# Remainders of the mixers' second-group weight pieces: VectorE in place of GpSimd

## The chip, the cores and the metric

The kernel runs on one core of one Trainium2 chip. A time is the device time of one execution in microseconds (us). Several executions are timed and their median is given; the profile is of one further execution, which has a time of its own.

## What is computed

The reference is one inference step of a decoder trunk with two layers (width 1024), for 1024 prompt tokens and 8 sample tokens that go through the same weights. Layer 0 mixes the tokens by dilated window attention, layer 1 by a pooling mixer. After each of them stands a gated channel mixer (ConvGLU) of hidden width 2816:

```python
def conv_glu(h, gate_prefix, w_in, conv_w, conv_b, w_out):
    u = h @ w_in
    gate, val = u[..., :D_FF], u[..., D_FF:]
    ext = jnp.concatenate([gate_prefix, gate], axis=1)
    S = h.shape[1]
    conv = conv_b + ext[:, 0:S] * conv_w[0]
    for j in range(1, CONV_WIDTH):
        conv = conv + ext[:, j:j + S] * conv_w[j]
    y = (jax.nn.silu(conv) * val) @ w_out
```

The pooling mixer takes trailing means over 2, 4, 8 and 16 tokens in four groups of channels, subtracts the token itself, and applies a linear map per group and a scale per channel. Every sub-layer begins with an RMSNorm and ends with a residual add. All is in float32.

## The kernel before

**Layout.** Channels lie on the 128 partitions, tokens on the free axis. The 1032 tokens are cut into chunks of 352, 336 and 344 columns (`CHUNKS`, line 21), and for the channel mixers into two groups (`GROUPS`, line 23): the first has chunks 0 and 1 (688 columns), the second has chunk 2 (344 columns: 336 prompt tokens and 8 sample tokens).

**Three products for one.** A float32 product is made of three matmuls in the fast float32 format: operands are split into a rounded part (`hi`) and the remainder (`lo`), and `accumulate` (line 115) adds hi·hi, hi·lo and lo·hi in PSUM.

**Weight pieces.** All weights come as one list of pieces of 128 x 1024 values (512 KB), in the order of use (line 56 on). SyncE's queue loads a piece into `w_raw` (line 88); ScalarE copies it to the rounded `w_hi` (line 99); GpSimd subtracts to make `w_lo` (line 100; two pieces at the very start are subtracted by VectorE, line 953); then the load of a later piece is issued, which goes into a buffer that the subtraction has released. `w_get` hands out the next piece, and `w_ahead(3)` splits pieces up to three ahead of the one in use. In the mixers there are four buffers each of `w_raw`, `w_hi` and `w_lo`, so that a new piece is split into the buffer that the piece four before it leaves.

**The channel mixers.** `steps` (lines 60 to 71) writes the order of their work out by hand: for each layer and each of the two groups, 22 up-projection steps `up`, of two pieces each (gate and value), with six `down` steps between them. The whole list of weights is gone through once for each group. In a step `up` (line 1079), a gate piece is multiplied with the normed tokens (`hh`, `hl`), ScalarE takes it out of PSUM (line 1097) and starts the convolution (line 1112), VectorE ends it (lines 1114 and, for the sample tokens, 1117), ScalarE applies SiLU (line 1101), VectorE multiplies with the value piece (line 1104), ScalarE rounds to `gh` (line 1105) and GpSimd subtracts to make `gl` (line 1106). A step `down` (line 1134) multiplies four (or two) such tiles with w_out, and VectorE adds the sums to the residual `xT` (line 1052). For the first group, a piece serves 24 matmuls in each of two chunks; for the second, 24 matmuls of 344 columns.

**What runs beside it.** `later` (line 166) puts small tasks of norms and of the pooling into a queue with due times in TensorE's modelled time, and `accumulate` sets them off between matmuls. So the order of each engine's instructions is fixed when the program is written, and each engine goes through its own in order. The pooling of chunks 0 and 1 (class `Pooling`, line 1166: `normed`, `sums`, `centred`, `high`, `low`; VectorE, with ScalarE for the rounding) is put in while layer 0's second group of tokens runs, with the costs of lines 1198 to 1203 as due times (modelled at one column of a matmul per 1/2400 us, line 122), and its projection (`project`, line 1262; two pieces) comes after the third `down` of that group.

Of the kernel before, what the change touches and what calls it, by code (L numbers as in the profile page):

```python
# [11 lines left out]
F32 = mybir.dt.float32  # L12
# [35 lines left out]
def trunk(ctx: ExitStack, tc: tile.TileContext, a, out):  # L48
    nc = tc.nc
# [6 lines left out]
    pieces = [a["w_qkv"][i] for i in range(72)] + [a["w_o"][h, i] for h in range(2) for i in range(4)]  # L56
# [4 lines left out]
    steps = []  # L61
# [9 lines left out]
        steps += [("up", x, 0) for x in halves[1:] if halves.index(x) == halves.index(at) + 1] + [("down", at, 5)]  # L71

    third = len(pieces) + 4
    for kind, (layer, _), which in steps:
        if kind == "up":
            pieces += [a["w_in"][layer, 2 * which + i] for i in range(2)]
        elif kind == "down":
            pieces += [a["w_out"][layer, DOWN[which][2] + i] for i in range(DOWN[which][1])]
        else:
            pieces += [a["w_pool"][i] for i in range(2)]  # L80
    raws, split, nxt, more = {}, {}, [0, 0, 0], [None]

    def w_load(n):
        while nxt[0] <= min(n, len(pieces) - 1):
            i = nxt[0]
            p = more[0] if i >= third and i % 4 > 1 else wpool
            raws[i] = p.tile([128, 1024], F32, name="w_raw", tag="w_raw", bufs=2)
            nc.sync.dma_start(out=raws[i], in_=pieces[i])
            nxt[0] += 1

    def w_split(n, eng=None, load=True):
        while nxt[1] <= min(n, len(pieces) - 1):
            i = nxt[1]
            w_load(i)
            p = more[0] if more[0] is not None and i % 4 > 1 else wpool
            hi = p.tile([128, 1024], F32R, name="w_hi", tag="w_hi", bufs=2)
            lo = p.tile([128, 1024], F32R, name="w_lo", tag="w_lo", bufs=2)
            raw = raws.pop(i)
            nc.scalar.activation(hi, raw, AF.Copy)  # L99
            (eng or nc.gpsimd).tensor_sub(lo, raw, hi.bitcast(F32))  # L100
            split[i] = (hi, lo)
            nxt[1] += 1
            if load:
                w_load(i + (4 if i >= third else 2))

    def w_get():
        i = nxt[2]
        nxt[2] += 1
        w_split(i)
        return split.pop(i)  # L110

    def w_ahead(k, load=True):
        w_split(nxt[2] - 1 + k, load=load)
# [168 lines left out]
    with ExitStack() as ph:  # L282
# [587 lines left out]
        for f in squares(0):  # L870
            f()
        w_split(0)
        ahead = squares(1)
        for f in ahead[:2] + [norms[0].stats, norms[0].spread] + ahead[2:6]:
# [537 lines left out]
```

## Time and profile before

| | |
|---|---|
| median of 3 runs | 2903.01 us (2902.28 to 2905.36) |
| time of the profiled execution | 2902.76 us |
| its span, first to last instruction | 2900.8 us |
| TensorE (PE) busy | 2786.3 us, 96% |
| VectorE (DVE) busy | 1629.2 us, 56% |
| ScalarE (ACT) busy | 1357.9 us, 47% |
| GpSimd (POOL) busy | 1409.8 us, 49% |
| of that, `w_lo` subtractions (line 100) | 848.5 us in 346 instructions |
| mean granted TensorE clock | 0.988 |

A row that says "A <- B" tells that A waited and that B ended the wait. L100 is line 100 of the kernel. PE is TensorE's matmuls and PEld its loads of weights into the array. A matmul's duration overlaps with that of its neighbours, so a row's mean for one matmul is more than its share of the time. The time of an execution is about 2 us longer than its span. Stretches are given in us from the start of the span.

### The profile page before, as it was taken

What the parts mean: (1) busy time and instruction counts of PE and PEld (TensorE: products, weight loads), DVE (VectorE), ACT (ScalarE), POOL (GpSimd) and SP (SyncE); (2) the same over time, 40 slices, a digit from 0 to 9 for tenths busy, and PEclk for the clock granted to TensorE, in tenths of its full rate; (3) what the DMA queues carried; (4) which work ended last, traced back from release to release, by engine and by line L of the source; (5) the groups of instructions that cost most, each with busy time, mean ns of one, the idle gap of its engine ahead of it and who ended that gap; (6) DMA issues with size and microseconds to landing.
All of it is one profiled execution on the core that took longest, in us unless ns stands there. A gap on an engine that the chain in (4) does not pass through costs nothing.

```text
span 2900.8 us, 46721 instructions
## 1 busy us (share of the span) xinstructions
PE 2786.3 (96%) x18109; PEld 2741.8 (95%) x18109; DVE 1629.2 (56%) x3196; ACT 1357.9 (47%) x2748; POOL 1409.8 (49%) x999
## 2 busy tenths in 40 slices
PE   6999999999999999999999999988899999999998
PEld 5999999999999999889999999988899999999998
DVE  6666756675666566765323334787756333435555
ACT  5565665566556655534222323445442333334443
POOL 4235443545354435445434434566753443445785
PEclk9999999999999999999999999999999999999999
DMA  3234333433343324438222222333332226223543
GB/s 117 58 85 124 95 86 87 122 90 91 82 128 94 87 86 145 139 95 106 67 73 73 66 73 73 109 103 108 119 103 66 73 67 81 67 72 98 182 139 102
DMA packets 203949, 277.80 MB, mean 96 GB/s; under 512 B 70272, under 2 KB 154096, under 8 KB 203728
## 3 DMA queue, kind: packets, MB, share of 16 engines
q1 hardware_dynamic: 203680, 274.80, 34.3%
q8 instruction: 142, 2.33, 0.3%
q14 instruction: 79, 0.65, 0.1%
q10 hardware_dynamic: 48, 0.02, 0.0%
HBM read 251.89 MB, written 23.34 MB: 95 GB/s over the span
## 4 chain that ended last, share of the span: by engine, by line
PE 77%; DVE 13%; ACT 3%; issue 3%; POOL 2%; DMA 1%; SPq 0%; DVEq 0%; ACTq 0%; POOLq 0%
PE mm L120 68%; PE o L489 2%; DVE k L408 2%; PE s L462 1%; POOL w_lo L100 1%; PE pt L475 1%; DVE conv L1117 1%; DVE conv L1114 1%; DVE x L399 1%; ACT w_hi L99 1%; PE s L455 1%; DVE x L397 1%; DVE sums L1225 1%; DVE sc L634 1%; PE spv L768 1%
## 5 line engine op out<-in xcount | busy, mean ns | idle before, releaser
L120 PE MATMUL mm<-hh,w_hi 128*128 128x352 f32 (+2 forms) x4064 | 1343.9, 331 | 13.9 <-ACT w_hi L99 6.9
L120 PE MATMUL mm<-hh,w_lo 128*128 128x352 f32 (+2 forms) x4064 | 1308.8, 322 | 10.4 <-POOL w_lo L100 10.4
L120 PE MATMUL mm<-hl,w_hi 128*128 128x352 f32 (+2 forms) x4064 | 1308.0, 322 | 2.4 <-DVE hl L255 2.4
L100 POOL TENSOR_TENSOR w_lo<-w_raw,w_hi 128x1024 fp32r<-128x1024 f32 x346 | 848.5, 2456 | 672.1 <-ACT w_hi L99 649.3
L120 PEld LDWEIGHTS mm<-hh,w_hi 128*128 128x128 f32 x4064 | 772.7, 190 | 20.7 <-ACT w_hi L99 7.5
L120 PEld LDWEIGHTS mm<-hh,w_lo 128*128 128x128 f32 x4064 | 771.2, 190 | 13.1 <-POOL w_lo L100 13.1
L120 PEld LDWEIGHTS mm<-hl,w_hi 128*128 128x128 f32 x4064 | 773.2, 190 | 4.7 <-DVE hl L255 3.9
L1114 DVE SCALAR_TENSOR_TENSOR conv<-gate,convp,conv 128x336 f32<-128x336 f32 (+1 forms) x176 | 253.6, 1441 | 428.6 <-ACT conv L1112 412.2
L99 ACT ACTIVATE w_hi<-w_raw 128x1024 fp32r<-128x1024 f32 x348 | 363.4, 1050 | 259.9 <-PE mm L120 240.1
L120 PE MATMUL mm<-gh,w_hi 128*128 128x352 f32 (+2 forms) x1056 | 340.8, 323 | 7.6 <-DVE conv L1104 6.3
L120 PE MATMUL mm<-gh,w_lo 128*128 128x352 f32 (+2 forms) x1056 | 340.1, 322 | 3.5 <-POOL w_lo L100 3.5
L120 PE MATMUL mm<-gl,w_hi 128*128 128x352 f32 (+2 forms) x1056 | 339.8, 322 | 0.6 <-POOL gl L1106 0.6
L1052 DVE TENSOR_TENSOR x<-x,mm 128x352 f32<-128x352 f32 (+2 forms) x312 | 157.1, 511 | 257.1 <-PE mm L120 256.5
L467 ACT ACTIVATE p<-p,st 128x128 f32<-128x128 f32 (+1 forms) x384 | 170.0, 443 | 202.4 <-DVE st L464 201.7
L1106 POOL TENSOR_TENSOR gl<-conv,gh 128x352 fp32r<-128x352 f32 (+2 forms) x132 | 124.5, 944 | 238.1 <-ACT gh L1105 233.4
L120 PEld LDWEIGHTS mm<-gh,w_hi 128*128 128x128 f32 x1056 | 199.6, 189 | 9.3 <-DVE conv L1104 7.6
L120 PEld LDWEIGHTS mm<-gh,w_lo 128*128 128x128 f32 x1056 | 200.1, 189 | 4.4 <-POOL w_lo L100 4.4
L120 PEld LDWEIGHTS mm<-gl,w_hi 128*128 128x128 f32 x1056 | 199.8, 189 | 1.1 <-POOL gl L1106 1.1
L480 DVE TENSOR_TENSOR phl<-pt,phl 128x512 fp32r<-128x512 f32 (+1 forms) x192 | 104.6, 545 | 164.2 <-ACT phl L479 163.1
L368 ACT ACTIVATE raw<-mm 128x336 f32<-128x336 f32 (+1 forms) x216 | 144.5, 670 | 102.5 <-PE mm L120 99.1
L1101 ACT ACTIVATE conv<-conv 128x688 f32<-128x688 f32 (+1 forms) x88 | 55.9, 635 | 275.1 <-DVE conv L1114 137.2
L1097 ACT ACTIVATE gate<-mm 128x352 f32<-128x352 f32 (+2 forms) x132 | 59.8, 454 | 224.1 <-PE mm L120 222.5
(190 smaller groups left out, 3190.3 us busy)
## 6 DMA issues: line engine op xcount, KB each, us to landing
w_raw<-in_w_in SPq DMA_DIRECT2D x176, 512.0 KB
w_raw<-in_w_out SPq DMA_DIRECT2D x88, 512.0 KB
w_raw<-in_w_qkv SPq DMA_DIRECT2D x72, 512.0 KB
x<-qd SPq DMA_DIRECT2D x48, 256.0 KB
kc<-in_cache_k SPq DMA_DIRECT2D x48, 256.0 KB
vc<-in_cache_v SPq DMA_DIRECT2D x48, 256.0 KB
x<-c_d SPq DMA_DIRECT2D x42, 256.0 KB
out_new_k<-raw SPq DMA_DIRECT2D x8, 516.0 KB
```

Source lines behind the costliest of these rows:

```text
L99: nc.scalar.activation(hi, raw, AF.Copy)
L100: (eng or nc.gpsimd).tensor_sub(lo, raw, hi.bitcast(F32))
L120: nc.tensor.matmul(ps, l, r, start=first and i == 0, stop=last and i == n - 1)
L368: nc.scalar.activation(stream(raw[:, :T], u.g, c0, t1, which > 0), ps[:, :w].rearrange("p (s r) -> p s r", r=DILS[u.g]), AF.Copy, scale=si ...
L408: nc.vector.tensor_copy(keys[h][own, 0, t], raw[own, t])
L467: nc.scalar.activation(p[:, h, :w], p[:, h, :w], AF.Exp, bias=u.st[:, i, h, 0:1], scale=-1.0, accum_out=u.st[:, i, h, 1:2])
L480: nc.vector.tensor_sub(phl[:, :, 1, :w], ps[:, :, :w], phl[:, :, 0, :w].bitcast(F32))
L489: nc.tensor.matmul(u.o[:, h, 128 * q:128 * (q + b1 - b0)], u.v[j // 4][:, j % 4, h, :], u.pt[j][0][:, h, x, 128 * b0:128 * b1], start=firs ...
L1052: nc.vector.tensor_add(xT[ct][:, c0:c1], xT[ct][:, c0:c1], ps)
L1097: nc.scalar.activation(gate[:, 2 + s:2 + e], group(tiles8(w, c), c), AF.Copy)
L1106: nc.gpsimd.tensor_sub(self.gl[f][:, s:e], conv[:, s:e], self.gh[f][:, s:e].bitcast(F32))
L1114: nc.vector.scalar_tensor_tensor(conv[:, :n], gate[:, j:j + n], cw[j], conv[:, :n], op0=ALU.mult, op1=ALU.add)
```

## The change

In the list of pieces, those that belong to steps of the second group of tokens (`half` is 1) are noted in a set, 130 in all: 64 for each layer, and the two of the projection that stands among layer 0's second-group steps. For these pieces `w_split` issues the subtraction of `w_lo` on VectorE; for all others it stays on GpSimd. The place of the instruction in the written order, its operands and buffers stay.

```diff
     third = len(pieces) + 4
-    for kind, (layer, _), which in steps:
+
+    quick = set()
+    for kind, (layer, half), which in steps:
+        begin = len(pieces)
         if kind == "up":
             pieces += [a["w_in"][layer, 2 * which + i] for i in range(2)]
         elif kind == "down":
             pieces += [a["w_out"][layer, DOWN[which][2] + i] for i in range(DOWN[which][1])]
         else:
             pieces += [a["w_pool"][i] for i in range(2)]
+        if half:
+            quick.update(range(begin, len(pieces)))
...
             nc.scalar.activation(hi, raw, AF.Copy)
-            (eng or nc.gpsimd).tensor_sub(lo, raw, hi.bitcast(F32))
+            (eng or (nc.vector if i in quick else nc.gpsimd)).tensor_sub(lo, raw, hi.bitcast(F32))
```

## Rows read from the trace of the kernel before

**Rows 1.** Windows: PE, PEld, DVE, ACT, POOL busy; granted clock, DMA, GB/s

```profile
1860.00:1902.00 42.00, 33.07 (x184) 31.55 (x184) 41.28 (x63) 14.03 (x19) 22.53 (x16) 0.91 0.29 87
1902.00:1932.00 30.00, 27.11 (x162) 25.98 (x161) 17.92 (x28) 14.16 (x21) 21.35 (x17) 0.96 0.38 114
1932.00:1980.00 48.00, 40.71 (x236) 39.16 (x235) 44.02 (x58) 18.96 (x27) 29.71 (x25) 0.89 0.35 104
2080.00:2120.00 40.00, 33.23 (x193) 32.37 (x193) 28.40 (x40) 21.49 (x34) 27.76 (x24) 0.91 0.35 110
2720.00:2860.00 140.00, 140.00 (x892) 139.98 (x891) 74.30 (x96) 63.14 (x89) 111.59 (x90) 1.00 0.47 147
1860.00:2120.00 260.00, 233.01 (x1399) 227.02 (x1399) 201.78 (x291) 118.98 (x180) 167.93 (x126) 0.95 0.37 112
```

**Rows 2.** What TensorE waited for, 1860 to 2120 us: total, times, longest

```profile
PE mm L120 <- POOL w_lo L100: 13.9, 12, 2.4
```

**Rows 3.** Timeline at 1837 us, VectorE and GpSimd: start, duration, instruction

```profile
1836.93 0.22 DVE L1117 SCALAR_TENSOR_TENSOR conv<-stT,convp,conv 128x8 f32<-128x8 f32 x1
1837.16 2.70 POOL L100 TENSOR_TENSOR w_lo<-w_raw,w_hi 128x1024 fp32r<-128x1024 f32 x1
1837.54 2.35 DVE L1117 SCALAR_TENSOR_TENSOR conv<-stT,convp,conv 128x8 f32<-128x8 f32 x1
```

**Rows 4.** VectorE groups of the pooling, 1860 to 2120 us: busy, mean ns

```profile
L1225 DVE TENSOR_TENSOR sums<-sums 128x704 f32<-128x704 f32 (+7 forms) x12 | 17.7, 1473 | 0.4
L1225 DVE TENSOR_TENSOR sums<-nrow 128x704 f32<-128x704 f32 (+7 forms) x8 | 9.4, 1169 | 0.0
L1242 DVE SCALAR_TENSOR_TENSOR nrow<-sums,nrow 128x704 f32<-128x704 f32 (+1 forms) x8 | 9.1, 1133 | 0.2
L1220 DVE COPY halo<-nrow 128x32 f32<-128x32 f32 x8 | 6.9, 864 | 0.0
L1210 DVE COPY nrow<-halo 128x32 f32<-128x32 f32 x8 | 4.2, 530 | 0.1
L1240 DVE TENSOR_TENSOR edge<-sums,consts 128x2 f32<-128x2 f32 (+3 forms) x4 | 2.5, 618 | 0.0
```

**Rows 5.** VectorE, two of these groups in 1860 to 1902 us alone

```profile
L1242 DVE SCALAR_TENSOR_TENSOR nrow<-sums,nrow 128x704 f32<-128x704 f32 x4 | 3.6, 893 | 0.1
L1210 DVE COPY nrow<-halo 128x32 f32<-128x32 f32 x4 | 0.7, 178 | 0.1
```

**Rows 6.** Timeline of ScalarE at 1868 us

```profile
1868.34 0.79 ACT L1254 ACTIVATE hh<-nrow 128x704 fp32r<-128x704 f32 x1 [6.19 <-DVE nrow L1245]
1869.04 2.00 ACT L99 ACTIVATE w_hi<-w_raw 128x1024 fp32r<-128x1024 f32 x2
```

**Rows 7.** GpSimd groups, 1860 to 1902 us

```profile
L100 POOL TENSOR_TENSOR w_lo<-w_raw,w_hi 128x1024 fp32r<-128x1024 f32 x8 | 21.1, 2650 | 8.6 <-ACT w_hi L99 8.6
L1106 POOL TENSOR_TENSOR gl<-conv,gh 128x344 fp32r<-128x344 f32 x2 | 2.4, 1195 | 6.5 <-ACT gh L1105 6.5
```

**Rows 8.** VectorE, convolution, 1860 to 1902, then 1932 to 1975 us

```profile
L1117 DVE SCALAR_TENSOR_TENSOR conv<-stT,convp,conv 128x8 f32<-128x8 f32 x2 | 2.5, 1266 | 0.0
...
L1114 DVE SCALAR_TENSOR_TENSOR conv<-gate,convp,conv 128x336 f32<-128x336 f32 x6 | 5.5, 914 | 0.9 <-ACT conv L1112 0.9
L1117 DVE SCALAR_TENSOR_TENSOR conv<-stT,convp,conv 128x8 f32<-128x8 f32 x6 | 3.4, 575 | 0.0
```

**Rows 9.** The two subtractions that VectorE makes: ns min, median, max

```profile
L100 DVE TENSOR_TENSOR w_lo<-w_raw,w_hi x2: 1224/1225/1226, 62.4 to 68.7; 128x1024 fp32r<-128x1024 f32 x2
```

**Rows 10.** Timeline of VectorE at 2030 us: one round of an up step

```profile
2030.62 1.71 DVE L1114 SCALAR_TENSOR_TENSOR conv<-gate,convp,conv 128x336 f32<-128x336 f32 x1 [2.68 <-ACT conv L1112]
...
2039.03 1.73 DVE L1114 SCALAR_TENSOR_TENSOR conv<-gate,convp,conv 128x336 f32<-128x336 f32 x1 [2.68 <-ACT conv L1112]
```

**Rows 11.** Waits of SP's DMA queue, 1860 to 2120 us

```profile
SPq L88 <- POOL w_lo L100: 217.7, 50, 15.5
```

**Rows 12.** VectorE, 2680 to 2860 us: the second layer's second group

```profile
L1117 DVE SCALAR_TENSOR_TENSOR conv<-stT,convp,conv 128x8 f32<-128x8 f32 x33 | 43.6, 1321 | 0.0
```

## Prediction

> **What bounds the kernel now.** I first read the busy shares in 40 slices: TensorE is at nine tenths or more nearly everywhere, so only stretches in which it falls back can give time. The second view is the windows. While layer 1's second group of tokens runs, TensorE is busy 140.0 of 140 us with 892 matmuls, 0.157 us each, at full clock; while layer 0's second group runs, from 1860 to 2120 us, it is busy 233.0 of 260 us with 1399 matmuls [rows 1]. At 0.157 us these would need 219.6 us. So 40.4 us are lost there: 27.0 idle, and 13.4 because the matmuls ran slower (granted clock 0.95 in the mean, 0.89 and 0.91 in the worst windows; the rows show it lower only in windows with idle time [rows 1], a mixture of 1.2 and 2.4 GHz). These 40.4 us are all that the change can win: in no other stretch with pieces that it moves does TensorE wait, but for the final norm at the very end.
>
> Third, the list of waits: 13.9 of the 27.0 us end when GpSimd delivers `w_lo` [rows 2]. That reads as if GpSimd were too slow, and its window shows 167.9 of 260 us busy [rows 1]. But the fourth view, the timeline, shows the cause behind it. A VectorE instruction of 8 columns (line 1117) takes 0.22 us while GpSimd runs only a tiny copy; the next one, issued while a `w_lo` subtraction is under way on GpSimd, takes 2.35 us, and ends at 1839.89, 0.03 us after that subtraction [rows 3]. VectorE is held until GpSimd is done. The fifth view, VectorE's groups, shows it all along: in the pooling (lines 1210 to 1245) copies of 32 columns have a mean of 0.86 or 0.53 us [rows 4] where unheld ones take 0.178 [rows 5]. So VectorE is 41.3 of 42 and 44.0 of 48 us busy in the two stretches in which the pooling of chunks 0 and 1 is put in [rows 1], a good part of it held. ScalarE goes down with it: its rounding of pooled rows waits 6.19 us for VectorE, and two `w_hi` stand behind it in its queue [rows 6]. Late `w_hi` makes late `w_lo`, and TensorE stops.
>
> **The change, part by part.**
>
> *Removed from GpSimd:* the subtractions of 130 pieces, some 2.65 us each here [rows 7]. GpSimd's own time is worth nothing directly; its hold on VectorE is. Held time in the two pooling stretches, as busy time less count times the unheld duration (0.893 us for 704 columns, 0.178 for 32 or fewer [rows 5]; 0.22 for line 1117 [rows 3]; 0.5 for 336 columns, an estimate on the line through the first two):
> - line 1225: 17.7 + 9.4 - 20 x 0.893 = 9.2 [rows 4]
> - line 1242: 9.1 - 8 x 0.893 = 2.0; line 1220: 6.9 - 8 x 0.178 = 5.5; line 1210: 4.2 - 1.4 = 2.8; line 1240: 2.5 - 0.7 = 1.8 [rows 4]
> - lines 1117 and 1114: 2.5 - 0.4, 3.4 - 1.3, 5.5 - 3.0 = 6.7 [rows 8]
>
> Together 28.0 us off VectorE.
>
> *Added to VectorE:* the same subtractions at 1.225 us, by the two that it makes now [rows 9]. GpSimd started 8 in 42 us [rows 7], as many in the second stretch; the due times of lines 1198 to 1203 spread a chunk's pooling over 21.4 us of modelled time, which at 24 x 344 / 2400 = 3.4 us a piece is 6 pieces. I take 7 each: 14 x 1.225 = 17.2 us. The trace shows no such instruction in VectorE's queue amid a backlog. Below, it costs no more than its 1.225 us, if the rounded part is always ready. Above, VectorE stands behind its `w_hi`, with all pooling, products and residual adds queued behind it, for as long as ScalarE needs for a pooled rounding and a `w_hi`: 0.79 + 1.0 = 1.8 us [rows 6]. I take nothing for most, since ScalarE is busy only 14.0 of 42 us [rows 1] and the pooling's tasks stand between; but for the gate piece of each up step the full wait, about 1.5 us (a rounding to `gh`, then a `w_hi`), as its subtraction comes directly behind the product that ScalarE must round first. Four such steps lie in these stretches, by their two and six instructions of line 1117 [rows 8], two a step: 6.0 us. VectorE's two stretches change by -28.0 + 17.2 + 6.0 = -4.8 us, and the idle time of TensorE in them, 8.9 + 7.3 us [rows 1], falls by as much: VectorE stays the bound there.
>
> *Outside the pooling,* 27.0 - 16.2 = 10.8 us of the idle time remain, most of it at 2080 to 2120 and 1902 to 1932 us [rows 1]. Here a backlog is worked off. One round of an up step takes 8.41 us, from one line 1114 to the next [rows 10], while TensorE needs 48 x 0.157 = 7.5 us. So rounds that are late stay late. Two held instructions a round, 1.71 us [rows 10] and 2.35 [rows 3] in place of 0.5 and 0.22, give back 3.3 us; two subtractions cost 2.45 us, of which the first falls into the 2.68 us in which VectorE now waits for ScalarE [rows 10]. The round becomes 8.41 - 3.3 + 1.2 = 6.3 us, at worst 7.6 if nothing overlaps. At 6.3 the backlog goes at a us per step, and I leave 1 us of the 10.8.
>
> *Loads.* SP's queue waits for the subtraction that frees a `w_raw`: 217.7 us in 50 waits [rows 11]. This wait moves to VectorE; with four buffers a load has some three pieces of lead, so I cost it at nothing. Without this cover TensorE would wait on `w_hi`.
>
> *Elsewhere.* In layer 1's second group the same trade takes place under a TensorE that never waits: line 1117 alone is held 43.6 - 33 x 0.22 = 36 us in 180 [rows 12]. VectorE is 74.3 of 140 us busy there [rows 1], and cover is ample. First-group pieces stay on GpSimd.
>
> *Sum.* Idle time saved 4.8 + 9.8 = 14.6 us. The slow clock goes with the idle time in proportion: 40.4/27.0 = 1.50, so 21.9 us. The profiled execution took 2902.8 us, 2.0 more than its span and 0.2 less than the median; 2903.0 - 22 = **2881 us**.
>
> **The rivals.**
>
> *GpSimd still holds VectorE.* `gl` stays on GpSimd, with 1.2 us each [rows 7], and a subtraction that falls behind one may wait for it. Four such waits, one for each up step of the pooling stretches, take back 4.8 us, and only the time outside is won: 9.8 x 1.5 = 15, **2888 us**. For it speaks that a `w_lo` is issued just when ScalarE has rounded `gh`, so at the same moment as `gl`; against it, that GpSimd is otherwise nearly free, so `gl` is early. The Trainium skill, "SBUF — State Buffer", "Who interferes with whom", says that a VectorE instruction with two inputs in SBUF and a GpSimd instruction that reads SBUF block each other, and that the one issued second waits for all of the first. By that rule the moved subtraction is itself open to the hold, the sum would be 2888, and [rows 3] agree with it.
>
> *The whole loss goes.* If the pooling's backlog stays within the lead that three pieces split ahead give, nothing is left of the 40.4 us: **2863 us**. For it: VectorE enters each stretch without the backlog of slow rounds, which I left out. Against: VectorE's work there stays as large as TensorE's.
>
> *No change.* Each of the 14 subtractions waits for a `w_hi` of 1.0 us [rows 6]: -4.8 + 14 = +9.2 in the pooling, which eats the 9.8 us from outside: **2903 us**.
>
> *Slower: VectorE's queue stands behind ScalarE.* Each of the 14 waits the upper 1.8 us. Then the pooling stretches grow by 25.2 - 4.8 = 20.4 us, less 9.8, times 1.5: 16 us, **2919 us**. It is slower by more than 0.2% (5.8 us, about what a measurement can tell) from 1.33 us a piece on. For it: ScalarE already waits for VectorE [rows 6], so each would wait for the other. Against: the two `w_hi` follow directly on the rounding, long before VectorE has gone through the next pooled pair.
>
> That the change does not do what it says I rule out: the set holds the numbers under which pieces are split, and all second-group pieces are in it.
>
> **How the numbers follow.** Forecast 0.48 (its own range 2870 to 2890), GpSimd still holds 0.14, whole loss goes 0.18, no change 0.13, slower 0.07. The range leaves out no more than the last two: 2860 to 2898 us. Faster by over 0.2%: 0.80; within: 0.13; slower: 0.07.
>
> **What would show it.** Right: line 1117 near 0.25 us in the second groups, 32-column copies near 0.2, `w_lo` on VectorE near 1.23, rounds of 7.5 us, TensorE idle some 12 us in the stretch after 1860 us, clock above 0.95. VectorE should still be near full in two pooling stretches. Wrong: line 1114 or 1225 as long as before (the hold has another source); `w_lo` instructions preceded by idle time "<- ACT w_hi" of a us or more each; TensorE waiting for VectorE's `w_lo` after 2660 us; or TensorE without a gap through the pooling.

## The result, and the profile after

The changed kernel takes 2877.95 us (median of 5 runs, 2875.72 to 2882.55) against 2903.25 us for the kernel before on the same chip (2902.28 to 2909.12): a ratio of 0.9907, 95% interval 0.9892 to 0.9922. It is faster by 25 us; 2881 us had been forecast, in a range of 2860 to 2898. The profiled execution's span is 2873.9 us, 26.9 less than before. One of the five executions of a later run, the one with the stretched pooling, took 8800.73 us, and is not counted in that run's ratio.

In the changed kernel the lines from 84 on have numbers higher by 5: the subtraction is line 105, the convolution's two instructions on VectorE are lines 1119 and 1122, the pooling's sums line 1230. Part 1 of its page, and the two groups of part 5 that make `w_lo`:

```profile
PE 2777.4 (97%) x18109; PEld 2736.4 (95%) x18109; DVE 1629.4 (57%) x3330; ACT 1361.1 (47%) x2748; POOL 1074.2 (37%) x865
...
L105 POOL TENSOR_TENSOR w_lo<-w_raw,w_hi 128x1024 fp32r<-128x1024 f32 x212 | 514.0, 2425 | 574.2 <-ACT w_hi L104 561.3
...
L105 DVE TENSOR_TENSOR w_lo<-w_raw,w_hi 128x1024 fp32r<-128x1024 f32 x136 | 166.7, 1226 | 87.6 <-ACT w_hi L104 87.5
```

134 subtractions went from GpSimd to VectorE (66 pieces a layer and two of the projection; the text ahead of the prediction counted 64, as the last `down` has four pieces and not two). GpSimd lost 335.6 us of work. VectorE took on 134 x 1.226 = 164 us and is busy 1629.4 us, against 1629.2 before: it got back as much as it was given. The next rows show where: its instructions are no longer held.

The groups of VectorE from 1860 to 2095 us, with busy time and mean ns, to be set beside [rows 4, 5]:

```profile
L105 DVE TENSOR_TENSOR w_lo<-w_raw,w_hi 128x1024 fp32r<-128x1024 f32 x52 | 63.6, 1225 | 27.8 <-ACT w_hi L104 27.8
...
L1230 DVE TENSOR_TENSOR sums<-sums 128x704 f32<-128x704 f32 (+7 forms) x12 | 10.6, 883 | 0.4
...
L1122 DVE SCALAR_TENSOR_TENSOR conv<-stT,convp,conv 128x8 f32<-128x8 f32 x34 | 7.5, 220 | 0.0
...
L1230 DVE TENSOR_TENSOR sums<-nrow 128x704 f32<-128x704 f32 (+7 forms) x8 | 7.1, 883 | 0.0
L1247 DVE SCALAR_TENSOR_TENSOR nrow<-sums,nrow 128x704 f32<-128x704 f32 (+1 forms) x8 | 7.0, 874 | 0.2
L1215 DVE COPY nrow<-halo 128x32 f32<-128x32 f32 x7 | 1.2, 178 | 0.1
L1225 DVE COPY halo<-nrow 128x32 f32<-128x32 f32 x7 | 1.2, 175 | 0.0
```

Every mean is now that of an unheld instruction: 883 ns where it was 1473 and 1169, 175 where it was 864. The subtractions themselves show no hold either (1225 ns in the mean, 1247 for the longest). What is new is the 27.8 us in which VectorE stands before a `w_lo` until ScalarE has made its `w_hi`.

The windows (columns as in [rows 1]) and, answering to [rows 2], the whole list of what TensorE waited for from 1860 to 2093 us:

```profile
1860.00:1900.00 40.00, 37.82 (x227) 36.97 (x226) 36.05 (x73) 15.91 (x22) 4.49 (x10) 0.96 0.30 93
1930.00:1970.00 40.00, 34.91 (x201) 33.68 (x200) 32.47 (x57) 17.69 (x26) 6.97 (x14) 0.91 0.36 115
1860.00:2100.00 240.00, 231.25 (x1443) 228.84 (x1442) 185.30 (x340) 121.26 (x181) 34.72 (x73) 0.98 0.39 122
2690.00:2830.00 140.00, 140.00 (x893) 139.98 (x892) 81.98 (x131) 63.48 (x88) 17.47 (x52) 1.00 0.50 150
```

```profile
PE mm L125 <- DVE w_lo L105: 3.7, 4, 1.9
PE mm L125 <- ACT gh L1110: 2.1, 1, 2.1
PE mm L125 <- DVE hl L260: 1.5, 1, 1.5
PE mm L125 <- ACT w_hi L104: 1.1, 1, 1.1
PE mm L125 <- POOL gl L1111: 0.3, 1, 0.3
```

TensorE is idle 8.75 us from 1860 to 2100 us, where it was 27.0. Its 1443 matmuls would take 226.6 us at 0.157 us, so 4.7 us go to the slower clock, where it was 13.4. Together 13.4 us are lost in place of 40.4: the 27.0 us between these are the whole difference of the spans. In layer 1's second group (2690 to 2830 us) nothing changed for TensorE.

### The profile page after: what moved, and what is told of

It is laid out like the page before. It is cut to its first block, busy times and chain, and to the rows that moved or that the text cites. A ratio compares the mean times of both kernels' runs of the same rounds, so it can differ in the third digit from the quotient of the medians.

```text
span 2873.9 us, 46685 instructions
## 1 busy us (share of the span) xinstructions
PE 2777.4 (97%) x18109; PEld 2736.4 (95%) x18109; DVE 1629.4 (57%) x3330; ACT 1361.1 (47%) x2748; POOL 1074.2 (37%) x865
## 5 line engine op out<-in xcount | busy, mean ns | idle before, releaser
L105 POOL TENSOR_TENSOR w_lo<-w_raw,w_hi 128x1024 fp32r<-128x1024 f32 x212 | 514.0, 2425 | 574.2 <-ACT w_hi L104 561.3
L1119 DVE SCALAR_TENSOR_TENSOR conv<-gate,convp,conv 128x336 f32<-128x336 f32 (+1 forms) x176 | 220.5, 1253 | 384.9 <-ACT conv L1117 375.9
L105 DVE TENSOR_TENSOR w_lo<-w_raw,w_hi 128x1024 fp32r<-128x1024 f32 x136 | 166.7, 1226 | 87.6 <-ACT w_hi L104 87.5
```

The source lines that it names most:

```text
L105: (eng or (nc.vector if i in quick else nc.gpsimd)).tensor_sub(lo, raw, hi.bitcast(F32))
L1119: nc.vector.scalar_tensor_tensor(conv[:, :n], gate[:, j:j + n], cw[j], conv[:, :n], op0=ALU.mult, op1=ALU.add)
```

## The experiments

Runs that were timed together share one set of times of the kernel before. One measure serves beside the median: in each trace, the time from the first start of line 1117 to the last of line 1278 (1122 and 1283 in the changed kernel), which holds layer 0's second group and ends in layer 1's first. It leaves out the attention before it, which varies: the first gate is taken out of PSUM at 1316.7 us in one profiled execution of the changed kernel and at 1326.4 in another. From mark to mark it is 2425.1 - 1790.5 = 634.6 us before and 2397.9 - 1790.1 = 607.8 us after; the second profiled execution of the changed kernel has 607.7.

**Which pieces matter: one layer at a time.**

```diff
-        if half:
+        if half and layer == 0:
             quick.update(range(begin, len(pieces)))
```

> Only layer 0's second-group pieces (with the projection's two) are subtracted by VectorE; layer 1's stay on GpSimd. Theory (the hold on VectorE costs time only where VectorE is the bound, in the stretch from 1860 to 2100 us): all of the gain stays, 2878 us, give or take 4. Rival (a shorter w_lo is worth something for every piece, and layer 1's 64 pieces carry half of it): about 2890 us.

Measured: 2879.45 us, ratio 0.9911 (0.9894 to 0.9928). The second run has `layer == 1` in the condition.

> Only layer 1's second-group pieces are subtracted by VectorE. Theory: TensorE never waits there, so 2903 us, within 4. Rival (every piece counts): about 2890 us.

Measured: 2903.68 us beside 2906.39 for the kernel before, ratio 0.9992 (0.9983 to 1.0001): no difference that can be told. From the first mark to the last it takes 634.9 us, and the run with layer 0 alone 607.8. So about half of the moved subtractions bring everything, and the other half nothing, although VectorE is held in layer 1 too. With layer 0 alone moved, line 1122 after 2500 us reads (ns min/median/max):

```profile
L1122 DVE SCALAR_TENSOR_TENSOR conv<-stT,convp,conv x44: 212/1279/2370, 2590.0 to 2850.0; 128x8 f32<-128x8 f32 x44
```

The hold is there, with a median of 1279 ns, under a TensorE that is busy 259.9 of the 260 us from 2590 to 2850; it costs nothing.

**The hold alone, without `w_lo` behind it.** In the changed kernel, GpSimd subtracts a second time after VectorE, into the used-up `w_raw`, so that `w_lo` comes from VectorE while GpSimd reads as long as before:

```diff
             (eng or (nc.vector if i in quick else nc.gpsimd)).tensor_sub(lo, raw, hi.bitcast(F32))
+            if i in quick:
+                nc.gpsimd.tensor_sub(raw, raw, hi.bitcast(F32))
```

> As the changed kernel, and GpSimd subtracts as well, w_raw - w_hi into w_raw, once VectorE has made w_lo; nobody uses that result, but the next load into this w_raw waits for it, as it did before. So w_lo comes from VectorE as in the changed kernel, and GpSimd reads SBUF as long as in the kernel before. Theory (the hold by a GpSimd subtraction is what cost the time): the held instructions are back (line 1122 at over 1 us in the mean), VectorE has them and the 1.2 us per piece too, and the kernel is slower than before, 2915 to 2960 us. Rival (the gain came from w_lo itself, which is ready in 1.2 in place of 2.4 us and no longer waits in GpSimd's queue): 2880 to 2890 us.

Measured: 2979.89 us, ratio 1.026 (1.0245 to 1.0275), slower than the kernel before by 74 us and than the changed one by 102. The rival falls. VectorE from 1860 to 2120 us, and GpSimd below it:

```profile
L105 DVE TENSOR_TENSOR w_lo<-w_raw,w_hi 128x1024 fp32r<-128x1024 f32 x46 | 73.7, 1603 | 21.7 <-ACT w_hi L104 21.7
L1121 DVE SCALAR_TENSOR_TENSOR conv<-gate,convp,conv 128x336 f32<-128x336 f32 x29 | 30.9, 1065 | 7.7 <-ACT conv L1119 7.5
L1232 DVE TENSOR_TENSOR sums<-sums 128x704 f32<-128x704 f32 (+7 forms) x12 | 18.9, 1572 | 0.4
...
L1124 DVE SCALAR_TENSOR_TENSOR conv<-stT,convp,conv 128x8 f32<-128x8 f32 x28 | 10.3, 369 | 0.0
```

```profile
L107 POOL TENSOR_TENSOR w_raw<-w_raw,w_hi 128x1024 f32<-128x1024 f32 x47 | 121.7, 2590 | 90.4 <-DVE w_lo L105 75.1 <-issue 7.4 <-DVE edge L1247 6.0
L1113 POOL TENSOR_TENSOR gl<-conv,gh 128x344 fp32r<-128x344 f32 x14 | 20.0, 1425 | 11.5 <-ACT gh L1112 11.5
```

The larger group of sums is back at 1572 ns. One thing was expected wrongly: the instruction of 8 columns (line 1124 here) has a mean of 369 ns, not over 1 us, because GpSimd's second subtraction starts at another point of the round, and so holds others: the larger convolution (1065 in place of 565) and the next `w_lo` (1603 in place of 1225). The time is also above the range that was given. From mark to mark 682.0 us are taken, 74.2 more than in the changed kernel; the other 28 us were lost after it, since VectorE, held and with the subtractions on top, is too slow for layer 1's second group as well (504.0 us from the last mark to the end of the span, 476.0 in the changed kernel; TensorE is busy 232.8 of the 250 us from 2700 to 2950).

**The same occupation of GpSimd, without reading.** The second subtraction is replaced by memsets of `w_raw`, at the same place in the order, with the same loads waiting for them:

```diff
             (eng or (nc.vector if i in quick else nc.gpsimd)).tensor_sub(lo, raw, hi.bitcast(F32))
+            if i in quick:
+                for w in (1024, 1024, 512):
+                    nc.gpsimd.memset(raw[:, :w], 0.0)
```

> As the run with the second subtraction, but in its place GpSimd only writes w_raw, with memsets of 1024, 1024 and 512 columns (by the rows of smaller memsets some 2.4 us together; an estimate): same place in its queue, same loads behind it, about the same time, but nothing read. Theory (it is the reading that holds VectorE): line 1122 stays at 0.22 us, and the time stays at 2878 us, give or take 5. Rival (GpSimd's occupied queue, behind which gl and the first two columns of the gate wait, is what cost the time): back to 2895 to 2905 us, with line 1122 at 0.22 us all the same. Second rival (writing holds VectorE too): as the other run.

Measured: 2881.56 us, ratio 0.9919 (0.9904 to 0.9934). GpSimd and VectorE from 1860 to 2100 us (the instruction of 8 columns is line 1125 here, the sums line 1233):

```profile
L108 POOL MEMSET w_raw<- 128x1024 f32 x159 | 128.6, 811 | 61.3 <-DVE w_lo L105 55.1
L1114 POOL TENSOR_TENSOR gl<-conv,gh 128x344 fp32r<-128x344 f32 x18 | 20.0, 1110 | 5.8 <-ACT gh L1113 5.8
```

```profile
L105 DVE TENSOR_TENSOR w_lo<-w_raw,w_hi 128x1024 fp32r<-128x1024 f32 x53 | 66.6, 1259 | 29.0 <-ACT w_hi L104 28.9
...
L1233 DVE TENSOR_TENSOR sums<-sums 128x704 f32<-128x704 f32 (+7 forms) x12 | 10.6, 884 | 0.4
...
L1125 DVE SCALAR_TENSOR_TENSOR conv<-stT,convp,conv 128x8 f32<-128x8 f32 x34 | 7.5, 221 | 0.0
...
L1218 DVE COPY nrow<-halo 128x32 f32<-128x32 f32 x8 | 4.5, 562 | 0.1
L1228 DVE COPY halo<-nrow 128x32 f32<-128x32 f32 x8 | 2.4, 300 | 0.0
```

Three memsets take 2.43 us (3 x 811 ns), as long as a subtraction, and `gl` and the gate's columns queue behind them as they did before the change. VectorE's instructions with two inputs are not held (221 ns, and 884 for the sums), and the kernel keeps all but some 3 us of the gain (610.6 us from mark to mark). Its small copies are still held, 562 and 300 ns in place of 178 and 175: so the second rival, that writing holds VectorE too, is true of the copies, and that cost little here. The hold run and this one differ in what GpSimd does in about the same time, a subtraction that reads two operands or memsets that only write, and they are 98 us apart: GpSimd's reading, with the hold on two-input instructions that comes with it, and not its occupied queue, is what cost the time. What part of the 25 us comes from `w_lo` itself, which is ready in 1.2 in place of 2.4 us, no run separates.

**The wait behind `w_hi`: is it a cost?** After each product of an up step VectorE stands 1.5 us before the next `w_lo`, as the prediction had it: 17 of the 52 subtractions of the stretch have such a wait. In this run that subtraction is written later:

```diff
             w = w_get()
-            w_ahead(3)
+            held = []
+            w_ahead(3, late=held)
...
             self.convolve(f, gate, conv, half)
+            for g in held:
+                g()
```

(`held` takes the subtraction and the load that follows it, for second-group pieces.) The changed kernel ran once more beside it.

> The changed kernel once more, to stand beside the three runs of this call: 2878 us, give or take 3.

Measured: 2877.49 us, ratio 0.9902 (0.9884 to 0.992).

> As the changed kernel, but in each up step of the second group the subtraction for the piece split ahead of the gate piece is written behind the step's convolution, so that VectorE no longer stands 1.5 us behind its w_hi directly after a product. Theory (in the pooling stretches VectorE is the bound, and these waits are part of what fills it, 6 us in the prediction's sum): the 1.5 us waits go, TensorE's idle time in the stretch falls from 8.8 us to about 4, and the time by 4 to 8 us, to 2870 to 2874 us. Rival (ScalarE sets the pace there: while VectorE waits, ScalarE makes the w_hi that is wanted anyway): 2878 us, and the wait shows up before another VectorE instruction.

Measured: 2879.6 us, ratio 0.9905 (0.9891 to 0.9918): no gain (607.3 us from mark to mark). The waits do go from before `w_lo` (27.8 us to 9.1), but the same ScalarE work is then waited for one instruction later, before the convolution (12.0 us to 32.4). The rival was right. A round after the first pooling stretch, in the run with the late subtraction and then in the changed kernel (VectorE's timeline):

```profile
1904.33 0.57 DVE L1129 SCALAR_TENSOR_TENSOR conv<-gate,convp,conv 128x336 f32<-128x336 f32 x1 [2.67 <-ACT conv L1127]
...
1905.57 2.35 DVE L109 TENSOR_TENSOR w_lo<-w_raw,w_hi 128x1024 fp32r<-128x1024 f32 x2
...
1911.01 0.57 DVE L1129 SCALAR_TENSOR_TENSOR conv<-gate,convp,conv 128x336 f32<-128x336 f32 x1 [2.67 <-ACT conv L1127]
```

```profile
1893.33 0.57 DVE L1119 SCALAR_TENSOR_TENSOR conv<-gate,convp,conv 128x336 f32<-128x336 f32 x1 [0.22 <-ACT conv L1117]
...
1897.72 1.25 DVE L105 TENSOR_TENSOR w_lo<-w_raw,w_hi 128x1024 fp32r<-128x1024 f32 x1 [1.51 <-ACT w_hi L104]
1898.89 0.57 DVE L1119 SCALAR_TENSOR_TENSOR conv<-gate,convp,conv 128x336 f32<-128x336 f32 x1
```

The round is 6.68 us with the late subtraction and 5.56 without: early, it runs while ScalarE prepares the convolution; late, it comes on top. TensorE's waits for `w_lo` rise from 3.7 to 9.5 us. The wait of 1.5 us is real, and moving it is worth nothing.

**More pieces.** All pieces of the mixers are subtracted by VectorE, the first group's too (`if half:` becomes `if True:`).

> The subtractions of all pieces of the mixers, the first group's too, by VectorE. In the first group a piece serves twice as many matmuls, so VectorE has 2.5 us more in each 15 us. Theory (a GpSimd subtraction costs where VectorE is the bound, nowhere else): TensorE's stall behind the pooling of chunk 2 (1.9 us idle, some 4 us with the slow clock) and a part of the stall at the first norm of the mixers (18 us with 12 us busy) go, 2868 to 2875 us. Rival (VectorE gets too much in the first group, where the convolution has 688 columns): slower than 2880 us, with TensorE waiting for w_lo from VectorE.

Measured: 2869.48 us, ratio 0.987 (0.9855 to 0.9885), the best of all runs but for those of the pacing below, which can't be told from it. From mark to mark 603.4 us, 4.4 less than in the changed kernel; where the rest of the 8 us between the medians lies, the traces don't show. The stall behind chunk 2's pooling is gone, from 2140 to 2200 us, in the changed kernel and then in this one:

```profile
2140.00:2200.00 60.00, 58.08 (x361) 57.78 (x360) 44.00 (x76) 18.71 (x27) 24.58 (x18) 0.97 0.22 71
```

```profile
2140.00:2200.00 60.00, 60.00 (x383) 59.70 (x382) 44.63 (x85) 18.27 (x25) 5.23 (x10) 1.00 0.25 77
```

22 more matmuls in the same 60 us, at full clock. At the first norm (1290 to 1330 us) TensorE is busy 35.1 us in place of 33.9. Both edits together:

> Both edits together. Theory: the gains add, 2862 to 2870 us. Rival: as the better of the two alone.

Measured: 2877.56 us, ratio 0.9896 (0.9882 to 0.9909). Neither expectation came true, and the gains don't add. It looks as if the late subtraction took back what the other edit gave, but the traces don't show that: from mark to mark the run takes 604.4 us, 1.0 more than with all pieces alone. Of the 6.2 us between the spans of the two profiled executions, 5.1 are there already at the mixers' first norm (1283.04 us against 1277.94, its first instruction on VectorE), which comes before all that the edits move.

**Is VectorE the bound in what is left?** The pooling's tasks are written over more of TensorE's time (`due[1] = cost * 1.7` in place of `1.2`).

> As the changed kernel, with the pooling's due times stretched by 1.7 in place of 1.2 (line 1208 of the changed kernel), so that a chunk's pooling is written over some 30 us of modelled time in place of 21. Theory (in the pooling stretches VectorE, not ScalarE or the loads, sets TensorE's pace, because more than its share is written into too short a stretch): the idle time of TensorE in the stretch from 1860 to 2100 us, 8.8 us, falls to 2 to 4 us, and the time by 6 to 10 us, to 2868 to 2872 us. Rival (the projection needs the pooled rows by then, so that later pooling only moves the wait to the projection): 2878 us or more, with TensorE waiting before the first matmul of the projection.

Measured: 2871.85 us, ratio 0.9872 (0.9854 to 0.989). From mark to mark 600.7 us, 7.1 less than in the changed kernel. From 1860 to 1900 us TensorE is now busy 39.9 of 40 us. The idle time in 1860 to 2100 us stays at 8.4 us all the same, since there are new waits just before the projection, in part where the rival put them (what TensorE waited for from 1290 to 2300 us, first row):

```profile
PE mm L125 <- DVE x L1057: 4.8, 3, 2.0
```

Of the three waits, two fall in the `down` step ahead of the projection (0.92 us at 1964.44, 1.81 at 1968.38), and the last, 2.05 us, at the projection's first matmul (1976.43). The stall behind chunk 2's pooling went as well. So both were right in part: the first pooling stretch was bound by VectorE and needed only more room; the second has a date to keep. The time came out as expected, but not by the idle time that was to fall to 2 to 4 us.

> The same with the subtractions of all pieces of the mixers by VectorE. Theory: the two gains add, 2860 to 2864 us. Rival: 2869 us, as without the stretching.

Measured: 2869.37 us, ratio 0.9868 (0.985 to 0.9886), the same as without the stretching. From mark to mark it is the shortest, 599.8 us, but both edits cure the stall behind chunk 2's pooling, so the gains overlap; what is left, 3.6 us from mark to mark, the medians don't show.

## Why the prediction was right

The direction, the place and the mechanism held, and the time came out 3 us below the forecast.

- *All that can be won is in one stretch.* Right: the runs by layer show all of the gain in layer 0's second group.
- *VectorE is held by GpSimd's subtraction.* Right, and shown by the pair of runs in which GpSimd reads or only writes.
- *Held time 28.0 us in the pooling.* Undersized by some 2.7 us: lines 1260 and 1245 were left out, and went from 9.6 to 7.5 and from 1.3 to 0.7 us. The estimate of 0.5 us for 336 columns measures 0.565.
- *14 subtractions, 17.2 us.* Oversized: the timeline has six in each stretch, 12 x 1.225 = 14.7 us. GpSimd started 8 in the first window and 10 in the second; that is not the count of those that stand between the pooling's instructions on VectorE.
- *Four waits of 1.5 us.* Each has the size that was forecast (1.50 and 1.51 us), but there are three, 4.5 us. The run with the late subtraction shows that moving it saves none of them.
- *VectorE's two stretches: -4.8 us.* With the three terms as measured: -30.7 + 14.7 + 4.5 = -11.5. From the first pooling copy until VectorE is ready for the next step's convolution, the first stretch went from 42.0 to 36.3 us (1860.06 to 1902.02, now 1856.84 to 1893.11); from the first copy to the product of line 1104, the second from 42.6 to 37.0 (1932.00 to 1974.61, now 1918.21 to 1955.24): 11.3 us less. TensorE's idle time in the two, 16.2 us before, is 7.3: it fell by 8.9, not by all of the 11.3. This is the term that was mis-sized: 4.8 us of idle time where 8.9 were won. All three parts erred to the same side, so no errors made up for each other.
- *Outside the pooling 1 us of 10.8 stays.* Right: 1.5 us, one wait at 2089.90. A round takes 5.56 us (6.3 forecast).
- *The clock in proportion, 1.50.* Right: 13.4 us lost to 8.75 idle is 1.53.
- *Layer 1, loads.* Right: SP's queue waits 174.9 us for VectorE's `w_lo` (1860 to 2093 us) in place of 217.7 for GpSimd's (1860 to 2120), and TensorE's list of waits has no load in it.

Of the rivals, that GpSimd's `gl` holds the moved subtraction fell with its mean of 1225 ns. Not because `gl` is early, as the prediction argued against it: `gl` runs in the very time in which VectorE waits for `w_hi` (from 1887.69 to 1888.62 us, while the subtraction starts at 1888.59). The whole loss did not go. The two cases without gain needed a wait at every piece; waits of 1.5 us, which the prediction also lists among the signs of being wrong, stand only at the gate pieces, as its sum has them, and moving them gained nothing. Their sums count the gate pieces' 6.0 us twice, once in the -4.8 and once in the 14 waits; without that they give 2893 and 2910 us.

## What to carry to other kernels

Look at the shortest and the mean duration of small VectorE instructions: where an instruction of 8 columns takes ten times its shortest time, as here, ask what holds its engine; busy shares hide it, as the hold counts as work. GpSimd's subtractions were free here only where VectorE had time to spare; a slower engine that "had room" was dearer than 1.2 us a piece on a busier one. Where the bound engine never waits, as in layer 1, the same hold costs nothing: cure it in the stretch that is short of time.

## What the runs showed of the hardware

The hold works in both directions. GpSimd's copy of 176 columns takes 0.34 us before (331 to 350 ns, line 1091) and 1.35 in the changed kernel, where it starts at 1832.09 us, just after a subtraction on VectorE, and ends with it, 0.2 us later (GpSimd's timeline, then VectorE's):

```profile
1832.09 1.35 POOL L1096 COPY gout<-stT 128x176 f32<-128x176 f32 x1
```

```profile
1832.00 1.24 DVE L105 TENSOR_TENSOR w_lo<-w_raw,w_hi 128x1024 fp32r<-128x1024 f32 x1 [1.50 <-ACT w_hi L104]
```

A GpSimd memset of 1024 columns (0.95 us in the median) does not hold VectorE's instructions with two inputs: beside 159 memsets the one of 8 columns keeps its 221 ns. It does hold the pooling's small copies on VectorE, which have one input. A copy of 30 columns that takes 0.18 us in the changed kernel takes 0.77 beside a memset that started before it, and ends 0.04 us after the memset (VectorE's timeline, then GpSimd's):

```profile
1896.31 0.77 DVE L1253 COPY nrow<-edge 128x30 f32<-128x30 f32 x1
```

```profile
1896.09 0.95 POOL L108 MEMSET w_raw<- 128x1024 f32 x1
```

In each of these cases, and in [rows 3], the instruction that started second waited. So the same GpSimd work at another point of the round held other instructions (the run with the second subtraction).
